# Row maxima off the diagonal by products of 64 rows in the two halves of the array, with the decay added on VectorE

## The chip, the cores and the metric

One core of one Trainium2 chip runs the whole program. The metric is the device time of one execution in microseconds; lower is better. Before the change it is 3023.38 us, the median of 3 runs (3023.07 to 3027.45).

## The reference, cut to what matters

Two decoder layers on a sequence of 2048 tokens, model width 1024: first a gated linear attention (GLA), then a forgetting attention (FoX) with 16 heads of width 64. The change lies in the second. For each head it computes, over all earlier keys,

```python
c = jnp.cumsum(log_f, axis=-1)
logits = (jnp.einsum('bhqd,bhkd->bhqk', qb, k).astype(jnp.float32) * scale
          + cb[..., :, None] - c[..., None, :])
mask = key_pos[None, :] <= q_pos[:, None]
probs = jax.nn.softmax(jnp.where(mask, logits, -jnp.inf), axis=-1)
return jnp.einsum('bhqk,bhkd->bhqd', probs.astype(v.dtype), v)
```

`log_f` is the logarithm of a forget gate, so `c` falls along the sequence. The softmax needs a number per query that is near the largest logit, to be subtracted ahead of the exponential. `c[t]` is the same for all keys of a query and drops out; what is left is the maximum over the keys of q.k - c[s].

## The kernel before, in words

**Tiling.** The sequence is cut into 4 blocks of 512 tokens (`T`, `NCH`). fp32 numbers are carried as two parts in a reduced fp32 format, high and low, and a dense product takes three matrix products (high x high, high x low, low x high). The second layer (from about 1100 us) runs block by block: projections, then for each of the 16 heads the maxima and the attention, then the output projection and a gated per-layer embedding.

**The maxima** (`maxima`, L1302). For block `c` and head `h` it goes over the key blocks `gk` = 0 to `c`, and in each over four query tiles `t` of 128. One product gives 128 queries x 512 keys: `E_` (128 x 512) is the stationary operand and `dk` the moving one. `E_` holds the high part of the queries in rows 0 to 63, ones in rows 64 and 65, and row 66 is filled later with the negative maximum; the rest is zero. `dk` holds the high part of the keys in rows 0 to 63 and the two parts of -c[s] in rows 64 and 65. So the product is q.k - c[s] at once. Off the diagonal (`gk < c`) VectorE reduces it with `tensor_reduce`; on the diagonal (`gk == c`) a fused add and maximum (`tensor_tensor_reduce`, in the profile CUSTOM_DVE_ANT_0 and a read of its accumulator) adds the mask `lim`. The four maxima per query are reduced, transposed on TensorE (`m4c` or `mx` with `ident`), negated and written by a DMA into row 66 of `E_`.

**The attention** (`attention`, L1364) uses the same `E_` again: for each tile of 128 keys one product of `B` (low and high part of the keys) with `A_` (high and low part of the queries) and one of `Dc` (rows as in `dk`, and a row of ones at 66) with `E_`. So the maximum comes off in the product. The exponentials follow on ScalarE, differences and sums on VectorE and GpSimd, and two products with `V`.

**Loads.** `load_d` (L1296) brings rows 64 to 129 of the scratch tensor `KS[gk][h]` (low part of the keys, high part, the two parts of the decay) into the 66 upper rows of one of two `Dm` (maxima) or two `Dc` (attention) tiles; `load_kv` (L1356) adds `B` and `V`. `forget` (L1220) computes the decay and stores its parts into `KS`. All DMAs are issued by SyncE (SP) in one queue.

**Order of the work.** Instructions are not emitted where they stand. A planner (`Streams`, L76) runs generators as streams with priorities: maxima 0.5, attention 2.5, dense work 3 (`P_M`, `P_A`, `P_D`, L60; the lower goes first). It keeps a clock of its own with a cost for each operation (`mm`, L397; `Engine`, L288), and a stream yields until operands, banks or marks are there by that clock. Each engine then executes in the planned order. The eight PSUM banks are handed out by `take` and `give`; `bank(keep)` (L252) waits until more than `keep` banks are free, and the maxima ask with `K_M` = 1. No product of the maxima is planned while the one before the last (`M_LIVE` = 2) is not yet reduced. `level(Q_M)` with 1 puts the reductions behind other work that VectorE could do.

**Weights** in the second layer come as already split halves of a matrix (`half`, L589: 12 products each) through `WB` + `WX` = 4 + 1 pairs of buffers (`wload`, L417); a load is issued when a pair falls free.

Every operation is recorded by one helper, so all rows of the trace have the line L180.

Of the kernel before, what the change touches and what calls it, by code (L numbers as in the profile page):

```python
# [20 lines left out]
P = 128  # L21
# [3 lines left out]
T = 512  # L25
# [8 lines left out]
PARTS = ("xnh", "xnl", "ogh", "ogl", "hr")  # L34


BANKS, K_D, K_V, K_M, M_LIVE = 8, 0, 0, 1, 2

PB, PF, PL, LAG = 3, 2, 3, 2

WR, WB, WX = 2, 4, 1

AB, A_STEP = 2, 8.0

# [9 lines left out]

G_OF = 2

Q_W, Q_C, Q_M = -1, 1, 1

Q_N = -1
P_A, P_M, P_D = 2.5, 0.5, 3  # L60
# [15 lines left out]
class Streams:  # L76
# [107 lines left out]
    @staticmethod  # L184
    def parts(ap):

        n = ap.tensor.name
        base = n.rsplit("_", 1)[0]
        if base in PARTS:
            first = ap.offset % (KT * T)  # L190
            last = first + sum((k - 1) * q for q, k in ap.ap[1:])
            return [(n, k) for k in range(first // T, last // T + 1)]
        if base[:2] == "KS":
            last = ap.offset + sum((k - 1) * q for q, k in ap.ap)
            return [(n, k) for k in range(ap.offset // (130 * T), last // (130 * T) + 1)]
        return [n]

    def over(self, ops):
# [117 lines left out]
def trunk_kernel(ctx: ExitStack, tc: tile.TileContext, a: dict, out: bass.AP, layers: int = 2):  # L316
# [77 lines left out]
    def t2(name, tag, bufs):  # L394
        return tmp.tile([P, T], F32, tag=tag, name=name, bufs=bufs)

    def mm(dst, w, x, start=True, stop=True):  # L397
        n = dst.free_size()
        sq_.op("P", [dst], [w, x], max(n, 64) * (4 if x.dtype == F32 or n < 256 else 1) / 2400.0 + 0.0134, partial(nc0.tensor.matmul, dst, w, x, start=start, stop=stop))

    def transpose(dst, src):
        sq_.op("P", [dst], [src], 0.107, partial(nc0.tensor.transpose, dst, src, ident))
# [1 line left out]
    def rdma(dst, src):  # L404
        nc.sync.dma_start(dst.bitcast(F32), src.bitcast(F32))
# [758 lines left out]
    def setup1():  # L1164
        sq_.flush()
        gx.close()
        f, fc = sbuf("f", 2), sbuf("fc", 1)
        L["f"] = f
        free.extend([fc.tile([P, 4, P], F32R, name=f"wx{x}{i}") for x in "hl"] for i in range(WX))

        L["onesb"] = fc.tile([P, P], F32R, name="onesb")
        onesb = L["onesb"].bitcast(F32)
        nc.vector.memset(onesb, 0.0)
        nc.vector.memset(onesb[0:64, 0:64], 1.0)
        nc.vector.memset(onesb[64:128, 64:128], 1.0)
        L["onesh"] = onesh = fc.tile([P, 2, P], F32, name="onesh")
        nc.vector.memset(onesh, 0.0)
        nc.vector.memset(onesh[:, 0, 0:64], 1.0)
        nc.vector.memset(onesh[:, 1, 64:128], 1.0)

        L["lim"] = lim = fc.tile([P, T + P], BF16, name="lim")
        nc.vector.memset(lim, 0.0)
        nc.vector.memset(lim[:, T:], -BIG)
        nc.gpsimd.affine_select(lim[:, T - P : T], lim[:, T - P : T], pattern=[[-1, P]], compare_op=ALU.is_ge, fill=-BIG, base=0, channel_multiplier=1)
        L["limT"] = limT = fc.tile([P, 2 * P], BF16, name="limT")
        nc.vector.memset(limT, 0.0)
        nc.gpsimd.affine_select(limT, limT, pattern=[[1, 2 * P]], compare_op=ALU.is_ge, fill=-BIG, base=-P, channel_multiplier=-1)
        L["qkg"] = qkg = fc.tile([P, 2], F32, name="qkg")
        nc.sync.dma_start(qkg, a["qkgain"])
        nc.vector.tensor_scalar(qkg[:, 0:1], qkg[:, 0:1], -(HD ** -0.5), None, ALU.mult)  # L1190
        nc.vector.tensor_scalar(qkg[:, 1:2], qkg[:, 1:2], -1.0, None, ALU.mult)
        L["bf"] = bf = fc.tile([FH, 1], F32, name="bf")
        nc.sync.dma_start(bf, a["fox_bf"])
        wfr = t2("wfr", "sq", 2)[:, 0 : KT * FH].rearrange("p (k n) -> p k n", n=FH)
        nc.sync.dma_start(wfr, a["fox_wf"])
        L["wf"] = wf = fc.tile([P, KT, 48], F32R, name="wf")
        nc.vector.memset(wf.bitcast(F32), 0.0)
        split(wf[:, :, 0:16], wf[:, :, 32:48], wfr, nc.vector)

        L["As"] = [fc.tile([P, T], F32R, name=f"As{i}") for i in range(NQ)]
        L["Es"] = [fc.tile([P, T], F32R, name=f"Es{i}") for i in range(NQ)]
        L["Dm"] = [fc.tile([P, T], F32R, name=f"Dm{i}") for i in range(2)]
        L["Dc"] = [fc.tile([P, T], F32R, name=f"Dc{i}") for i in range(2)]
        for t in (*L["Es"], *L["Dm"], *L["Dc"]):
            nc.vector.memset(t[64:128].bitcast(F32), 0.0)
        for t in L["Dc"]:
            rdma(t[66:67].rearrange("o (t n) -> o t n", n=P), ones[0:4])
        for t in L["Es"]:  # L1210
            nc.vector.memset(t[64:66].bitcast(F32), 1.0)
        L["carry"] = fc.tile([FH, 1], F32, name="carry")
        nc.vector.memset(L["carry"], 0.0)

        L["KS"] = [dram.tile([FH, 130, T], F32R, name=f"KS{c}") for c in range(NCH)]

        L["QS"] = [[dram.tile([P, T], F32R, name=f"QS{h}_{c}") for c in range(NCH)] for h in range(FH)]
        L["VS"] = [[dram.tile([8, P, 4, P], F32R, name=f"VS{i}_{c}") for c in range(NCH)] for i in range(2)]

    def forget(c):  # L1220
# [19 lines left out]
        nc.vector.scalar_tensor_tensor(cl, e, -1.0, ch.bitcast(F32), ALU.mult, ALU.subtract)  # L1240
        rdma(L["KS"][c][:, 128], ch)
        rdma(L["KS"][c][:, 129], cl)

    def qk_unit(c, u, col):

# [50 lines left out]
    def load_d(h, gk, kind):  # L1296
        d = L[kind][nd[kind] % len(L[kind])]
        nd[kind] += 1
        rdma(d[0:66], L["KS"][gk][h, 64:130])
        return d  # L1300

    def maxima():  # L1302

        done = []
        for i in range(NCH * FH):
# [3 lines left out]
            if i >= NQ:  # L1309
                yield ("S", i - NQ)  # L1310
            A_, E_ = L["As"][i % NQ], L["Es"][i % NQ]
            rdma(E_[0:64], L["QS"][h][c][0:64])
            rdma(A_, L["QS"][h][c])
            dk = load_d(h, 0, "Dm")
            mx = L["f"].tile([P, 4, NCH], F32, tag="mx", name="mx")
            for gk in range(c + 1):
                nxt = load_d(h, gk + 1, "Dm") if gk < c else None
                for t in range(4):
                    yield both(at(E_, dk), done[-M_LIVE] if len(done) >= M_LIVE else lambda: 0.0)
                    yield bank(K_M)  # L1320
                    n = T if gk < c else max(256, (t + 1) * P)
                    pm = psa("pm")
                    mm(pm[:, :n], E_[:, t * P : (t + 1) * P], dk[:, :n])
                    m1 = mx[:, t, gk : gk + 1]
                    with level(Q_M):
                        if gk < c:
                            nc.vector.tensor_reduce(m1, pm, AX.X, ALU.max)
                        else:
                            l0 = T - (t + 1) * P
                            nc.vector.tensor_tensor_reduce(pm[:, :n], pm[:, :n], L["lim"][:, l0 : l0 + n], 1.0, -BIG, ALU.add, ALU.max, accum_out=m1)  # L1330
                    give(pm)
                    done.append(at(mx))
                    yield
                dk = nxt
            if c:
                m4 = L["f"].tile([P, 4], F32, tag="m4c", name="m4c")
                nc.vector.tensor_reduce(m4, mx[:, :, : c + 1], AX.X, ALU.max)
# [6 lines left out]
            mr = L["f"].tile([4, P], F32R, tag="mr", name="mr")  # L1344
            nc.scalar.mul(mr, pt[0:4, 0:P], -1.0)
            give(pt)
            rdma(E_[66:67].rearrange("o (t n) -> o t n", n=P), mr)
            mark(("C", i))

    pend = []  # L1350
# [2 lines left out]
    def both(f, g):  # L1353
        return lambda: max(f(), g())
# [289 lines left out]
```

## Time and profile before

| what | value |
|---|---|
| median of 3 runs | 3023.38 us |
| the profiled execution, its time | 3025.52 us |
| its span, first to last instruction | 3023.8 us |
| granted TensorE clock, mean | 0.994 of full speed |
| TensorE busy | 2970.6 us (98%) |
| VectorE / ScalarE / GpSimd busy | 2134.2 / 1905.4 / 1330.8 us |
| moved by DMA | 648.15 MB, 66.5% of 16 engines |

Rows name an engine (PE is TensorE, PEld its loads of weights, DVE VectorE, ACT ScalarE, POOL GpSimd, SP the DMA queue), then what is written and read by the program's names without buffer numbers; every PSUM tile is called `bank`. Products are given as rows*columns of the weights and the shape of the moving operand.

### The profile page before, as it was taken

The numbers are of one execution on the slowest core, as the hardware profiler recorded it, in microseconds if no ns is written. First come the engines' busy times: TensorE is split into PE (matmuls) and PEld (weight loads), VectorE is DVE, ScalarE is ACT, GpSimd is POOL, SyncE is SP. The second block draws the span as 40 slices with busy tenths as digits, with TensorE's granted clock in tenths as the row PEclk, the third lists the DMA queues.
The fourth block names the chain that finished last, engine by engine and source line by source line (L and its number), as shares of the span: only waits on it lengthen the run. The fifth ranks groups of instructions, "written<-read, shape, count | busy, mean of one in ns | idle before, by whom it ended". The sixth has DMA issues, their size and how long they took to land.

```text
span 3023.8 us, 43646 instructions
## 1 busy us (share of the span) xinstructions
PE 2970.6 (98%) x13568; PEld 2406.8 (80%) x13568; DVE 2134.2 (71%) x3824; ACT 1905.4 (63%) x3651; POOL 1330.8 (44%) x1097
## 2 busy tenths in 40 slices
PE   8999999999999999999899999999999999999998
PEld 6887887888788888887788777778777788777876
DVE  7687668668765765675764877774787768798845
ACT  6666666657565465664555756565776657667745
POOL 1232222213222234453543645553776647677741
PEclk9999999999999999999999999999999999999999
DMA  5565657556642568887668777667776777766665
GB/s 193 180 212 192 203 195 244 196 186 228 209 143 81 179 196 250 276 268 248 218 220 270 236 247 246 213 211 257 226 219 224 230 238 233 227 190 210 196 228 159
DMA packets 379738, 648.15 MB, mean 214 GB/s; under 512 B 43097, under 2 KB 78433, under 8 KB 379506
## 3 DMA queue, kind: packets, MB, share of 16 engines
q1 hardware_dynamic: 379506, 645.37, 66.5%
q8 instruction: 108, 1.77, 0.2%
q14 instruction: 124, 1.02, 0.1%
HBM read 521.86 MB, written 123.21 MB: 213 GB/s over the span
## 4 chain that ended last, share of the span: by engine, by line
PE 90%; DVE 3%; ACT 3%; DMA 2%; issue 1%; POOL 0%; SPq 0%; DVEq 0%; ACTq 0%; POOLq 0%
PE bank L180 90%; ACT rs L180 1%; DMA B<-KS 1%; DVE wl L180 0%; DVE hr L180 0%; DMA Dm<-KS 0%; DMA wr<-gla_wv 0%; DVE ny L180 0%; ACT Ph L180 0%; DVE bank L180 0%; SPq L180 0%; DVE rs L180 0%; POOL Pl L180 0%; DMA ar<-fox_wg 0%; DMA hr<-hs 0%
## 5 line engine op out<-in xcount | busy, mean ns | idle before, releaser
L180 ACT ACTIVATE Ph<-bank 128x512 fp32r<-128x512 f32 (+2 forms) x640 | 339.0, 545 | 131.1 <-PE bank L180 64.2
L180 DVE TENSOR_TENSOR wl<-wr,wh 128x512 fp32r<-128x512 f32 x332 | 253.4, 770 | 149.8 <-ACT wh L180 120.7
L180 PE MATMUL bank<-xnh,wh 128*128 128x512 f32 (+1 forms) x1184 | 338.7, 393 | 0.3 <-DVE ny L180 0.2
L180 PE MATMUL bank<-xnh,wl 128*128 128x512 f32 (+1 forms) x1184 | 337.7, 392 | 0.0
L180 PE MATMUL bank<-xnl,wh 128*128 128x512 f32 (+1 forms) x1184 | 333.0, 391 | 0.0
L180 DVE TENSOR_REDUCE mx<-bank 128x1 f32<-128x512 f32 x384 | 253.2, 684 | 79.4 <-PE bank L180 76.7
L180 ACT CAST wh<-wr 128x512 fp32r<-128x512 f32 x332 | 202.6, 615 | 106.4 <-PE bank L180 63.1
L180 DVE TENSOR_TENSOR Pl<-bank,Ph 128x512 fp32r<-128x512 f32 (+1 forms) x320 | 194.2, 607 | 106.4 <-ACT bank L180 95.4
L180 POOL TENSOR_TENSOR ag<-ag,Pf 128x512 f32<-128x512 f32 x192 | 226.4, 1179 | 79.2 <-ACT Pf L180 57.1
L180 PEld LDWEIGHTS bank<-xnh,wh 128*128 128x128 f32 x1184 | 220.3, 188 | 47.3 <-issue 1.1
L180 PEld LDWEIGHTS bank<-xnh,wl 128*128 128x128 f32 x1184 | 220.6, 188 | 45.7 <-issue 0.6
L180 PEld LDWEIGHTS bank<-xnl,wh 128*128 128x128 f32 x1184 | 219.9, 188 | 45.0 <-issue 0.9
L180 PE MATMUL bank<-ogh,wh 128*128 128x512 f32 x856 | 242.3, 393 | 5.2 <-ACT ogh L180 2.6
L180 PE MATMUL bank<-As,B 128*128 128x512 f32 (+2 forms) x640 | 241.1, 377 | 3.2 <-DMA B<-KS 1.0
L180 PE MATMUL bank<-ogl,wh 128*128 128x512 f32 x856 | 241.3, 393 | 0.3
L180 PE MATMUL bank<-ogh,wl 128*128 128x512 f32 x856 | 240.6, 392 | 0.0
L180 PE MATMUL bank<-Pl,V 128*128 128x512 f32 (+2 forms) x640 | 235.9, 369 | 2.8 <-POOL Pl L180 2.0
L180 PE MATMUL bank<-Ph,V 128*128 128x512 f32 (+2 forms) x640 | 235.0, 367 | 0.0
L180 PE MATMUL bank<-Es,Dc 128*128 128x512 f32 (+2 forms) x640 | 234.7, 367 | 0.0
L180 PE MATMUL bank<-Dm,Es 128*128 128x512 f32 (+2 forms) x640 | 231.1, 378 | 3.0 <-DMA Dm<-KS 2.4
L180 POOL TENSOR_TENSOR Pl<-Pf,Ph 128x512 fp32r<-128x512 f32 x192 | 228.8, 1197 | 2.7 <-ACT Ph L180 2.1
L180 PEld LDWEIGHTS bank<-ogh,wh 128*128 128x128 f32 x856 | 160.2, 189 | 40.3 <-ACT ogh L180 3.6
(271 smaller groups left out, 7072.8 us busy)
## 6 DMA issues: line engine op xcount, KB each, us to landing
B<-KS SPq DMA_DIRECT2D x160, 256.0 KB
V<-VS SPq DMA_DIRECT2D x160, 256.0 KB
Dm<-KS SPq DMA_DIRECT2D x160, 132.0 KB
Dc<-KS SPq DMA_DIRECT2D x160, 132.0 KB
wr<-gla_wv SPq DMA_DIRECT2D x64, 256.0 KB
wr<-gla_wqk SPq DMA_DIRECT2D x64, 256.0 KB
wr<-gla_wg SPq DMA_DIRECT2D x64, 256.0 KB
wr<-gla_wo SPq DMA_DIRECT2D x64, 256.0 KB
```

The costliest lines, as they stand in the source:

```text
L180: q.emit()
```

## The change

Off the diagonal two query tiles are taken together. The queries of one lie in rows 0 to 63 of `A_` (the high part, loaded there for the attention anyway), those of the other in rows 64 to 127 of `E_`; so `E_` and `dk` are turned over: high parts in rows 64 to 127, ones, decay and maximum in rows 0 to 2. `dk` gets the high part of the keys in both halves. Each product then has 64 rows, and the two use different halves of the array and different banks. They hold q.k alone; -c[s] is stored once per block in fp32 (`CS`), loaded as a tile broadcast to 128 partitions (`cb`, two buffers), and added by the fused add and maximum. Diagonal tiles stay as they are, but their loads, and those of the attention, take two DMAs in place of one. `KS` has a 131st row of zeros. To make room for `cb` the fifth pair of weight buffers goes (`WX` = 0). `M_LIVE`, `K_M` and `Q_M` change, and the planner counts the second product of a pair as 0.01 us.

```diff
-BANKS, K_D, K_V, K_M, M_LIVE = 8, 0, 0, 1, 2
+BANKS, K_D, K_V, K_M, M_LIVE = 8, 0, 0, 0, 3
...
-WR, WB, WX = 2, 4, 1
+WR, WB, WX = 2, 4, 0
...
-Q_W, Q_C, Q_M = -1, 1, 1
+Q_W, Q_C, Q_M = -1, 1, 0
...
-    def mm(dst, w, x, start=True, stop=True):
+    def mm(dst, w, x, start=True, stop=True, beside=0):
         n = dst.free_size()
-        sq_.op("P", [dst], [w, x], max(n, 64) * (4 if x.dtype == F32 or n < 256 else 1) / 2400.0 + 0.0134, partial(nc0.tensor.matmul, dst, w, x, start=start, stop=stop))
+        sq_.op("P", [dst], [w, x], 0.01 if beside else max(n, 64) * (4 if x.dtype == F32 or n < 256 else 1) / 2400.0 + 0.0134, partial(nc0.tensor.matmul, dst, w, x, start=start, stop=stop))
...
-            nc.vector.memset(t[64:128].bitcast(F32), 0.0)
+            nc.vector.memset(t[0:64].bitcast(F32), 0.0)
         for t in L["Dc"]:
-            rdma(t[66:67].rearrange("o (t n) -> o t n", n=P), ones[0:4])
+            rdma(t[2:3].rearrange("o (t n) -> o t n", n=P), ones[0:4])
...
-        L["KS"] = [dram.tile([FH, 130, T], F32R, name=f"KS{c}") for c in range(NCH)]
+        L["KS"] = [dram.tile([FH, 131, T], F32R, name=f"KS{c}") for c in range(NCH)]
+        for c in range(NCH):
+            rdma(L["KS"][c][:, 130], L["Dm"][0][0:FH])
+
+        L["CS"] = [dram.tile([FH, T], F32, name=f"CS{c}") for c in range(NCH)]
...
+        nc.vector.tensor_scalar(lf, e, -1.0, None, ALU.mult)
+        nc.sync.dma_start(L["CS"][c], lf)
...
     def load_d(h, gk, kind):
         d = L[kind][nd[kind] % len(L[kind])]
         nd[kind] += 1
-        rdma(d[0:66], L["KS"][gk][h, 64:130])
+        rdma(d[64:128], L["KS"][gk][h, 64:128])
+        n = 3 if kind == "Dm" else 2
+        rdma(d[0:n], L["KS"][gk][h, 128 : 128 + n])
         return d
+
+    def load_m(c, h, gk):
+
+        if gk == c:
+            return load_d(h, gk, "Dm"), None
+        d = L["Dm"][nd["Dm"] % len(L["Dm"])]
+        nd["Dm"] += 1
+        for i in range(2):
+            rdma(d[64 * i : 64 * i + 64], L["KS"][gk][h, 64:128])
+        cb = L["f"].tile([P, T], F32, tag="cb", name="cb", bufs=2)
+        nc.sync.dma_start(cb, L["CS"][gk][h : h + 1].to_broadcast([P, T]))
+        return d, cb
...
-            rdma(E_[0:64], L["QS"][h][c][0:64])
+            rdma(E_[64:128], L["QS"][h][c][0:64])
             rdma(A_, L["QS"][h][c])
-            dk = load_d(h, 0, "Dm")
+            nxt = load_m(c, h, 0)
...
             for gk in range(c + 1):
-                nxt = load_d(h, gk + 1, "Dm") if gk < c else None
+                dk, cb = nxt
+                nxt = load_m(c, h, gk + 1) if gk < c else None
+                if gk < c:
+
+                    for t in (0, 2):
+                        yield both(both(at(E_, dk), at(A_, cb)), done[-M_LIVE] if len(done) >= M_LIVE else lambda: 0.0)
+                        pms = []
+                        for j in range(2):
+                            yield bank(K_M * (1 - j))
+                            pms.append(psa("pm"))
+                        for j, q in enumerate((A_, E_)):
+                            js = slice(64 * j, 64 * j + 64)
+                            mm(pms[j], q[js, (t + j) * P : (t + j + 1) * P], dk[js], beside=j)
+                        for j, pm in enumerate(pms):
+                            with level(Q_M):
+                                nc.vector.tensor_tensor_reduce(pm, pm, cb, 1.0, -BIG, ALU.add, ALU.max, accum_out=mx[:, t + j, gk : gk + 1])
+                            give(pm)
+                            done.append(at(mx))
+                        yield
+                    continue
...
-            rdma(E_[66:67].rearrange("o (t n) -> o t n", n=P), mr)
+            rdma(E_[2:3].rearrange("o (t n) -> o t n", n=P), mr)
```

## Rows read from the trace of the kernel before

**Rows 1.** The page, part 1: busy time, share of span, instructions.

```profile
PE 2970.6 (98%) x13568; PEld 2406.8 (80%) x13568; DVE 2134.2 (71%) x3824; ACT 1905.4 (63%) x3651; POOL 1330.8 (44%) x1097
```

**Rows 2.** The page, part 4: the chain that ended last, by engine.

```profile
PE 90%; DVE 3%; ACT 3%; DMA 2%; issue 1%; POOL 0%; SPq 0%; DVEq 0%; ACTq 0%; POOLq 0%
```

**Rows 3.** Stretches: length, busy time of each engine, TensorE clock, DMA share, GB/s.

```profile
1180.00:2900.00 1720.00, 1700.66 (x7599) 1362.44 (x7597) 1246.73 (x2490) 1116.15 (x2236) 993.81 (x823) 1.00 0.74 232
2500.00:2800.00 300.00, 296.57 (x1321) 237.42 (x1320) 258.77 (x486) 214.60 (x431) 216.66 (x176) 1.00 0.69 214
```

**Rows 4.** Timeline of TensorE from 2003.96 us: start, time, engine, operation, count.

```profile
2003.96 0.39 PE L180 MATMUL bank<-Pl,V 128*128 128x512 f32 x1
2003.96 0.42 PEld L180 LDWEIGHTS bank<-Dm,Es 128*128 128x128 f32 x2
2004.19 0.62 PE L180 MATMUL bank<-Dm,Es 128*128 128x512 f32 x2
...
2004.65 0.40 PE L180 MATMUL bank<-As,B 128*128 128x512 f32 x1
```

**Rows 5.** VectorE's groups by form: count, busy us, mean ns, idle before.

```profile
L180 DVE TENSOR_REDUCE mx<-bank 128x1 f32<-128x512 f32 x384 | 253.2, 684 | 79.4 <-PE bank L180 76.7
...
L180 DVE SCALAR_TENSOR_TENSOR rs<-bank,rs 128x512 f32<-128x512 f32 x127 | 87.1, 686 | 1.6
...
L180 DVE CUSTOM_DVE_ANT_0 bank<-bank,lim 128x512 f32<-128x512 f32 x64 | 44.6, 697 | 5.3 <-PE bank L180 5.0
...
L180 DVE DVE_READ_ACCUMULATOR2_ANT mx<- 128x1 f32 x256 | 35.7, 139 | 0.2
```

**Rows 6.** TensorE's groups by form: products of the maxima with 512 columns.

```profile
L180 PE MATMUL bank<-Dm,Es 128*128 128x512 f32 x448 | 173.4, 407 | 2.9 <-DMA Dm<-KS 2.4 <-ACT rs L180 0.4
```

**Rows 7.** Timeline of the weight loads from 1808.43 us, beside products of 256 columns.

```profile
1808.43 0.19 PEld L180 LDWEIGHTS bank<-Es,Dc 128*128 128x128 f32 x1
1808.55 0.19 PEld L180 LDWEIGHTS bank<-Ph,V 128*128 128x128 f32 x1
1808.67 0.19 PEld L180 LDWEIGHTS bank<-Pl,V 128*128 128x128 f32 x1
```

**Rows 8.** Timeline of TensorE around weights of 48 and of 4 columns.

```profile
1806.11 1.79 PE L180 MATMUL bank<-xnh,wf 128*48 128x512 f32 x7
1807.74 0.40 PE L180 MATMUL bank<-Ph,V 128*128 128x512 f32 x1
...
1920.66 0.39 PE L180 MATMUL bank<-Pl,V 128*128 128x512 f32 x1
...
1920.89 0.27 PE L180 MATMUL bank<-ident,m4c 128*4 128x128 f32 x1
...
1920.92 0.36 PE L180 MATMUL bank<-As,B 128*128 128x256 f32 x1
```

**Rows 9.** Instructions on tile mx: the plain reductions, ns, first and last start.

```profile
L180 DVE TENSOR_REDUCE mx<-bank x384: 672/681/693, 1422.8 to 2854.7; 128x1 f32<-128x512 f32 x192
```

**Rows 10.** DMA queue (packets, MB, share), issues with KB, and issue times (ns).

```profile
q1 hardware_dynamic: 379506, 645.37, 66.5%
...
Dm<-KS SPq DMA_DIRECT2D x160, 132.0 KB
Dc<-KS SPq DMA_DIRECT2D x160, 132.0 KB
...
L180 SPq DMA_DIRECT2D Dm<-KS x160: 288/350/1011, 1097.7 to 2845.3; - x160
```

**Rows 11.** TensorE's waits for the maxima's keys; DMA pieces of the chain (start, us).

```profile
  DMA Dm<-KS: 4.8, 4
...
1922.74 7.08 DMA Dm<-KS
2391.22 5.24 DMA wl<-fox_wv_0l
2396.48 6.95 DMA B<-KS
```

More of the change, by code (lines that the diff above doesn't have):

```diff
@@ L194, in parts @@
             last = ap.offset + sum((k - 1) * q for q, k in ap.ap)
-            return [(n, k) for k in range(ap.offset // (130 * T), last // (130 * T) + 1)]
+            return [(n, k) for k in range(ap.offset // (131 * T), last // (131 * T) + 1)]
         return [n]
@@ L1206, in setup1 @@
         for t in (*L["Es"], *L["Dm"], *L["Dc"]):
-            nc.vector.memset(t[64:128].bitcast(F32), 0.0)
+            nc.vector.memset(t[0:64].bitcast(F32), 0.0)
         for t in L["Dc"]:
-            rdma(t[66:67].rearrange("o (t n) -> o t n", n=P), ones[0:4])
+            rdma(t[2:3].rearrange("o (t n) -> o t n", n=P), ones[0:4])
         for t in L["Es"]:
-            nc.vector.memset(t[64:66].bitcast(F32), 1.0)
+            nc.vector.memset(t[0:2].bitcast(F32), 1.0)
         L["carry"] = fc.tile([FH, 1], F32, name="carry")
         nc.vector.memset(L["carry"], 0.0)
-        L["KS"] = [dram.tile([FH, 130, T], F32R, name=f"KS{c}") for c in range(NCH)]
+        L["KS"] = [dram.tile([FH, 131, T], F32R, name=f"KS{c}") for c in range(NCH)]
+        for c in range(NCH):
+            rdma(L["KS"][c][:, 130], L["Dm"][0][0:FH])
+        L["CS"] = [dram.tile([FH, T], F32, name=f"CS{c}") for c in range(NCH)]
         L["QS"] = [[dram.tile([P, T], F32R, name=f"QS{h}_{c}") for c in range(NCH)] for h in range(FH)]
@@ L1320, in maxima @@
                     yield bank(K_M)
-                    n = T if gk < c else max(256, (t + 1) * P)
+                    n = max(256, (t + 1) * P)
                     pm = psa("pm")
                     mm(pm[:, :n], E_[:, t * P : (t + 1) * P], dk[:, :n])
-                    m1 = mx[:, t, gk : gk + 1]
                     with level(Q_M):
[L1326 to L1330, printed above, removed]
+                        l0 = T - (t + 1) * P
+                        nc.vector.tensor_tensor_reduce(pm[:, :n], pm[:, :n], L["lim"][:, l0 : l0 + n], 1.0, -BIG, ALU.add, ALU.max, accum_out=mx[:, t, gk : gk + 1])
                     give(pm)
@@ L1333, in maxima @@
                     yield
-                dk = nxt
             if c:
```

## The prediction

> **What bounds the kernel now.** I read the shares of the engines first, then the chain of work that ended last, then the stretches. TensorE is busy 98% of the span with 13,568 products and every other engine is well below it [rows 1]; the chain is 90% TensorE, and VectorE, ScalarE, the DMAs and plain issue hold about a tenth of it between them [rows 2]. The stretch from 1180 to 2900 us, where the changed work lies, shows the same: TensorE 1700.7 of 1720 us, VectorE 1246.7, the DMA engines 74% [rows 3]. The one place where a second engine comes near is 2500 to 2800 us: VectorE 258.8 of 300 us [rows 3]. A busy TensorE need not be a full one, so I looked at the distance between starts: a 512-column product occupies its slot for 0.23 us, although its own record is 0.39 us long [rows 4]; the rest of the record runs beside the next product. 13,568 products in 2970.6 us are 0.219 us each, so the engine is close to its own rate and fewer slots should mean less time. The clock is at its upper level in all of it (1.00 in both stretches of [rows 3]).
>
> All durations below are of the profiled execution: its time is 3025.52 us, 2.1 us above the median of 3023.38. What a run of this kernel can tell from no change is about 0.2%, 6 us.
>
> **1. The products.** Off the diagonal there are 384 of them: that is the count of plain reductions [rows 5], and the 448 products of 512 columns are these and the 64 last tiles of diagonals [rows 6]. 384 x 0.23 = 88 us of TensorE. They become 192 pairs of products with 64 rows, one in the upper and one in the lower half of the array. No product of the trace has fewer than 128 rows, so a pair has to be bounded.
> - *Best:* both run side by side and a pair takes one slot: 192 x 0.23 = 44 us less.
> - *Weights decide:* each half still loads its own 128 columns of weights. Where products are short (256 columns), products with a load each follow each other every 0.12 us [rows 7], so a load needs no more than that. If the second half's load starts only when the first product has started, the pair takes 0.12 + 0.23 = 0.35 us instead of 0.46: 0.11 x 192 = 21 us less.
> - *Nothing overlaps:* 0.
> - *Worse:* on each change between whole and half array the running product must end first, which is its record less its slot, 0.39 - 0.23 = 0.16 us, twice per pair: 0.23 + 0.32 = 0.55 us against 0.46, 17 us more; without any overlap on top of it 61 us more.
>
> I take 0.27 us per pair, 0.04 above one slot. Two loads at 0.12 us fit into the slot of the product ahead, which starts a load at its own start [rows 4], so the value lies nearer the best end. Saved: (0.46 - 0.27) x 192 = 36.5 us, all on the path.
>
> Does a change of the array's shape cost? The trace has a relative of it in the other direction, columns: seven products with 48 columns of weights start at 1806.11, and the next with 128 at 1807.74, 0.233 us each with both changes in it; the transposition with 4 columns starts 0.23 us after its forerunner and the next product 0.03 us after it [rows 8]. No change shows 0.16 us. The Trainium skill says otherwise: "TensorEngine Tiling (Array Packing)", section "Tiling Modes" (Key Properties), states that changing the tiling mode drains TensorE, and by it the sum would be the worse end above. The trace does not agree for columns; for rows no run here shows it. The other page, "TensorE: Matmul & The Clock Gate" (Part 3), starts packed products about 4 ns apart; by that a pair would cost almost exactly one slot and the sum would come out some 7 us lower.
>
> **2. VectorE.** A plain reduction is 684 ns. The diagonal already does the new form, add and maximum in one pass: 697 ns for 128x512, and 139 ns to read the accumulator [rows 5]. So 836 - 684 = 152 ns more, x384 = 58 us. The second operand is now fp32 and not bf16; a pass over 512 fp32 elements of a bank with an fp32 tile from SBUF is 686 ns [rows 5], so that costs nothing. The cover is TensorE's chain: VectorE goes from 1247 to about 1305 of 1720 us. VectorE holds 3% of the chain with 71% busy, 91 of 2134 us or 4%: 58 x 0.04 = 2.5 us. In 2500 to 2800 us the cover is thin: 86% busy already, and the new work (its share by time is 12 us, 300/1432 of 58, from 1423 to 2855 us [rows 9]) brings it to 90%. Half of those 12 us on the path would be 6. I take 4 us, between 0 and 10. The price falls on those queued behind a longer pass, chiefly ScalarE's exponentials, which wait for VectorE's mask on the diagonal.
>
> **3. DMAs and SP's queue.** 96 key blocks lie off the diagonal. Each now loads 2 x 128 KB of keys instead of 132 KB, and 256 KB for the broadcast decay: 380 KB x 96 = 37 MB on 645 MB [rows 10], all inside 1720 us at 74%; that takes the DMA engines to about 81%. The queue gains 96 second halves, 96 broadcasts, a second short load for each of 160 attention blocks and 64 diagonal blocks, and 8 stores: 424 issues of about 0.35 us [rows 10], 148 us in a queue whose issues are in order; weights and value tiles queue behind them. A key load takes some 7 us when the queue is full, and TensorE waited 4 times, 4.8 us in all, for one [rows 11]. With a tenth more traffic and each head's first key block some 0.7 us later in the queue (two more issues), I take 4 us; bounds 0, where the loads stay ahead as now, and 12, where the 48 heads with blocks off the diagonal each wait 0.25 us more.
>
> **4. One weight buffer less.** Five pairs of buffers become four in the second layer. Each serves 12 products, 12 x 0.23 = 2.8 us of unbroken dense work, so a load that starts when a buffer falls free has 3 x 2.8 = 8.3 us instead of 11 before its first use. Loads that are waited for took 5.2 to 7.1 us [rows 11]; 8.3 still covers that, barely, and attention lies between the dense products. I take 3 us; 0 where the cover holds, 10 where one in ten of the layer's 400 halves of a weight matrix (100 for each of four blocks, by the code) comes 0.25 us late.
>
> **5. The bookkeeping.** Looser limits on banks (a third reduction may be pending, no bank is kept back) and a planner that counts the second half of a pair as 0.01 us reorder the whole second layer. I put this at 0, within 5 either way. Setup (fills, four 32 KB zero rows) lies ahead of the layer once: under 1 us.
>
> **Sum.** -36.5 + 4 + 4 + 3 = -25.5 us: 3000 for the profiled execution, 2998 against the median.
>
> **Rivals.**
> - *The array empties at each change* (slower). The place is the first product of each pair and the first after it; it decides from 0.115 us per change on, where 0.23 + 2 x 0.115 = 0.46 eats the whole gain. At 0.16 us: 17 + 11 (points 2 to 4) = 28 us more, 3051. For it: no 64-row product was ever timed here. Against it: the narrow products [rows 8]. Chance 0.11. The skill's page on tiling, named above, is on this side.
> - *The halves do not run side by side*, so the change does not do what it says: 0 + 11, 3034. For it: the products stay two instructions in one stream. Chance 0.11.
> - *Weights decide*: -21 + 11, 3013. For it: loads are single file in the trace. Chance 0.13.
> - *The gain turns into waits*: TensorE is relieved, and VectorE's 2500 to 2800 us, the weights and the key loads pay their upper bounds, 10 + 12 + 10 = 32 us, which leaves 3019 at 36.5 saved. Chance 0.10.
> - The forecast: 0.55, 2978 to 3010.
>
> **How the numbers follow.** The low end is the best pair with the side costs at nothing, 3023.4 - 44 = 2979, and a little for the order, 2977; the high end takes in the halves that do not overlap, 3034, and leaves out the emptying array. Faster by over 0.2%: forecast and weights, less a little, 0.66. Slower: the first two rivals, 0.22. Within: the fourth and what the others leave, 0.12.
>
> **What would show it.** Right: products with 64 rows that start in twos a few hundredths of a us apart, the next whole product some 0.27 us after the first; VectorE about 58 us busier; TensorE's busy time in 1423 to 2855 us down by 30 to 40 us; TensorE's waits for DMA no more than a few us longer. Wrong: a gap of 0.1 us or more at the edges of each pair (emptying); second halves 0.12 us (weights) or 0.23 us (no overlap) behind the first; TensorE idle behind weights or maxima.

## The result and the profile after

The changed kernel takes 3215.61 us (median of 4 runs, 3209.07 to 3221.69) against 3025.20 for the kernel before on the same chip: 1.063 times as long, 95% interval 1.0618 to 1.0642. That is 190 us slower, on the other side of the forecast and far above its range. The profiled execution took 3218.49 us.

First the page of the changed kernel: busy time of each engine, the DMA queue, the chain by engine, and three groups of DMA issues.

```profile
PE 3066.8 (95%) x13568; PEld 2391.1 (74%) x13568; DVE 2140.5 (67%) x4212; ACT 1907.6 (59%) x3651; POOL 1322.3 (41%) x1097
...
q1 hardware_dynamic: 402962, 682.61, 68.0%
...
PE 79%; DMA 6%; DVE 5%; ACT 4%; issue 3%; POOL 3%; SPq 1%; DVEq 0%; POOLq 0%; ACTq 0%
...
Dm<-KS SPq DMA_DIRECT2D x256, 128.0 KB
cb<-CS SPq DMA_DIRECT2D x96, 256.0 KB
Dc<-KS SPq DMA_DIRECT2D x160, 128.0 KB
```

Against [rows 1]: the span grew by 193 us, from 3023.8 to 3216.8. TensorE's busy time grew by 96 us, and the time in which it does nothing from 53 to 150 us, another 97. No other engine works noticeably longer: VectorE has 2140.5 us against 2134.2. Against [rows 2] the chain lost 11 points of TensorE, and they went to everything at once: DMA (2 to 6%), POOL (0 to 3%), DVE (3 to 5%) and plain issue (1 to 3%). So the answer is not one engine that became too busy. The DMA engines carry the predicted 37 MB more (682.6 against 645.4 in [rows 10]) in a longer span.

The same stretches as in [rows 3] (length, busy time of each engine, TensorE's clock, DMA share, GB/s), then the mean clock of the whole span:

```profile
1180.00:2900.00 1720.00, 1624.97 (x6890) 1222.75 (x6889) 1130.89 (x2577) 997.60 (x1998) 866.99 (x725) 0.97 0.77 233
2500.00:2800.00 300.00, 283.77 (x1187) 207.67 (x1184) 215.00 (x486) 181.14 (x360) 172.70 (x140) 0.98 0.79 237
```

```profile
core 0: 3216.8 us, clock 0.977
```

In the same 1720 us TensorE does 6890 products where it did 7599. The clock was 0.994 of full speed over the span before and is 0.977 now. Of 3216.8 us that is (1 - 0.977) x 3216.8 = 74 us lost to the lower of the two levels (1.2 GHz in place of 2.4), against (1 - 0.994) x 3023.8 = 18 us before: up to 56 of TensorE's 96 us of additional busy time can be products that ran at the lower level.

**Who is waited for.** The two largest sums of TensorE's waits ahead of products on tile Dm, by what ended them (us, times):

```profile
  DMA Dm<-KS: 21.1, 16
  DVE mx L180: 13.7, 14
```

Before, TensorE's products waited 2.4 us for these loads, in 2 waits ([rows 6]; the 4.8 us in 4 waits of [rows 11] count the idle time ahead of the loads of weights too). DMAs of all kinds now end 42 us of TensorE's waits, 3 us before; most of the rest of the 97 us is ended by other engines, VectorE (39 against 17) and GpSimd (23 against 2) first. In the chain of waits 15 pieces of over 4 us are now loads of keys (the list of before names two of them, one in [rows 11]), 87 us in all against 12.5. One of the 15 (start, us, what), and TensorE at its end (in brackets idle time and what ended it):

```profile
2026.27 7.56 DMA Dm<-KS
```

```profile
2030.94 0.50 PE L180 MATMUL bank<-Dm,As 64*128 64x512 f32 x1
2033.87 0.49 PE L180 MATMUL bank<-Dm,Es 64*128 64x512 f32 x1 [2.43 <-DMA Dm<-KS]
```

The first product of the pair needs the half of the key tile that is loaded first, the second product the other half. Of TensorE's 16 waits for keys 14 stand, like this one, ahead of the second product of a head's first pair, and none ahead of the first.

**The place.** These loads sit where one head's maxima end and the next head's begin. SP's queue at such a place (start, us):

```profile
2082.70 0.45 SPq L180 DMA_DIRECT2D Dm<-KS  x1
2083.25 0.53 SPq L180 DMA_DIRECT2D cb<-CS  x1
2083.88 0.66 SPq L180 DMA_DIRECT2D Es<-mr  x1
...
2086.69 1.03 SPq L180 DMA_DIRECT2D Dm<-KS  x1
```

TensorE there, the last 512-column maxima product of the old head and the first of the new one:

```profile
2077.62 0.39 PE L180 MATMUL bank<-Dm,Es 128*128 128x512 f32 x1
...
2091.51 0.50 PE L180 MATMUL bank<-Dm,As 64*128 64x512 f32 x1
```

The first half of the key tile is issued at 2082.70, the second 4.0 us later at 2086.69, and the head's first product follows 13.9 us after the last one of the head before. The queue issued six other DMAs between the two. The reason stands in the planner's `Streams.op`: `Dm` is one operand for it, and a DMA ("H") that writes an operand is planned behind the landing of an earlier DMA that writes it,

```python
deps[o] = self.AFTER[o.e] if o.e != e or e == "H" else 0.0
```

What used to be one load of 66 rows is now two loads in series. I measured this gap, from the start of the last maxima product of a head to the first of the next, at all 45 such boundaries of blocks 1 to 3 (a head of block c has 4(c+1) of these products in a row): the median went from 9.3 to 15.0 us and the sum from 616 to 828 us.

**The pairs.** TensorE around one pair, products and loads of weights (start, us):

```profile
1995.55 0.84 PE L180 MATMUL bank<-xnl,wh 128*128 128x512 f32 x3
1996.32 0.50 PE L180 MATMUL bank<-Dm,As 64*128 64x512 f32 x1
1996.32 0.50 PE L180 MATMUL bank<-Dm,Es 64*128 64x512 f32 x1
1996.75 0.50 PE L180 MATMUL bank<-xnl,wh 128*128 128x512 f32 x1
1997.09 1.09 PE L180 MATMUL bank<-xnh,wl 128*128 128x512 f32 x4
```

```profile
1996.32 0.18 PEld L180 LDWEIGHTS bank<-Dm,As 64*128 64x128 f32 x1 [0.35 <-DVE ny L180]
1996.32 0.18 PEld L180 LDWEIGHTS bank<-Dm,Es 64*128 64x128 f32 x1
1996.75 0.19 PEld L180 LDWEIGHTS bank<-xnl,wh 128*128 128x128 f32 x1 [0.25 <-issue]
1996.86 0.89 PEld L180 LDWEIGHTS bank<-xnh,wl 128*128 128x128 f32 x4
```

The halves do run side by side: both start at 1996.32. But their weights are loaded at 1996.32 too, and those of the next whole product at 1996.75, with their own products; before, a load began one slot early [rows 4]. Both are the rule: in the median a load starts 2 ns ahead of its product for a pair behind whole products and for a whole product behind a pair, and 224 ns ahead for a whole product behind another. Over all 192 pairs the medians are: product ahead to pair 0.319 us, half to half 0.004, pair to the next product 0.422, and from that to the one after it 0.338. From the product ahead of the pair to the second behind it that is 1.089 us. Four whole products in a row take 4 x 0.23 = 0.92. A pair costs about 0.16 us more than the two products that it replaces, not 0.19 less.

### The profile page after: what moved, and what is told of

It is laid out like the page before. It is cut to its first block, busy times and chain, and to the rows that moved or that the text cites. A ratio compares the mean times of both kernels' runs of the same rounds, so it can differ in the third digit from the quotient of the medians.

```text
span 3216.8 us, 44816 instructions
## 1 busy us (share of the span) xinstructions
PE 3066.8 (95%) x13568; PEld 2391.1 (74%) x13568; DVE 2140.5 (67%) x4212; ACT 1907.6 (59%) x3651; POOL 1322.3 (41%) x1097
## 4 chain that ended last, share of the span: by engine, by line
PE 79%; DMA 6%; DVE 5%; ACT 4%; issue 3%; POOL 3%; SPq 1%; DVEq 0%; POOLq 0%; ACTq 0%
PE bank L180 79%; DMA Dm<-KS 3%; POOL Pl L180 1%; DVE bank L180 1%; ACT Ph L180 1%; SPq L180 1%; DVE ny L180 1%; POOL ag L180 1%; ACT rs L180 1%; DMA wh<-ple_gate_1h 0%; ACT bank L180 0%; DVE hr L180 0%; DVE wl L180 0%; POOL ogl L180 0%; ACT sq L180 0%
## 5 line engine op out<-in xcount | busy, mean ns | idle before, releaser
L180 PE MATMUL bank<-xnh,wh 128*128 128x512 f32 (+1 forms) x1352 | 387.7, 395 | 2.8 <-DVE ny L180 2.0
L180 PE MATMUL bank<-xnl,wh 128*128 128x512 f32 (+1 forms) x1352 | 384.8, 394 | 0.0
L180 PE MATMUL bank<-xnh,wl 128*128 128x512 f32 (+1 forms) x1352 | 384.0, 394 | 0.0
L180 DVE CUSTOM_DVE_ANT_0 bank<-bank,cb 128x512 f32<-128x512 f32 x384 | 260.3, 703 | 92.5 <-PE bank L180 90.0
L180 PEld LDWEIGHTS bank<-xnh,wh 128*128 128x128 f32 x1352 | 252.4, 189 | 60.4 <-issue 4.7
L180 PEld LDWEIGHTS bank<-xnl,wh 128*128 128x128 f32 x1352 | 251.8, 189 | 56.2 <-issue 6.0
L180 PEld LDWEIGHTS bank<-xnh,wl 128*128 128x128 f32 x1352 | 251.6, 189 | 54.8 <-issue 4.2
L180 PE MATMUL bank<-ogh,wh 128*128 128x512 f32 x960 | 272.2, 397 | 6.4 <-ACT wh L180 2.6
L180 PE MATMUL bank<-ogl,wh 128*128 128x512 f32 x960 | 269.7, 394 | 0.3
L180 PE MATMUL bank<-Es,Dc 128*128 128x512 f32 (+2 forms) x640 | 243.5, 381 | 15.6 <-DMA Es<-mr 11.7
L180 PEld LDWEIGHTS bank<-ogl,wh 128*128 128x128 f32 x960 | 180.1, 189 | 41.0 <-issue 2.2
```

Source lines behind the costliest of these rows:

```text
L180: q.emit()
```

## The experiments

The runs began with four theories: the planner's new rules, the pairs, the traffic, or the missing weight buffer makes it slow. VectorE's pass joined them at run 4 and the late keys at run 8. All ratios are to the kernel before on the same chip.

**1. Rules of before in the changed kernel.**

```diff
-K_M, M_LIVE = 0, 3      Q_M = 0
+K_M, M_LIVE = 1, 2      Q_M = 1
```

> The changed kernel with the old rules of the planner (K_M 1, M_LIVE 2, Q_M 1), all else as changed. Theory rules (TensorE stalls because the planner hands out the last bank and VectorE is late with it): at least half of the 190 us comes back, 3120 us or less. Theories pair, traffic and weight buffer: within 30 us of the changed kernel's 3216.

3312.78 us, 1.0956 (1.0922 to 1.0989): 97 us worse than the change, outside both expectations. With the rest of the change in place, the new rules are the better ones.

**2. The kernel before without the fifth pair of weight buffers.**

```diff
-WR, WB, WX = 2, 4, 1
+WR, WB, WX = 2, 4, 0
```

> The kernel before with four pairs of weight buffers in place of five, nothing else. Theory weight buffer: it takes a large part of the 190 us, 3080 us or more. The other theories: at most 20 us more than before, 3045 or less.

3018.40 us (8 runs), 0.9976 (0.9964 to 0.9987): 7 us faster. The buffer was worth nothing.

**3. Whole products in the changed kernel.** Loads, broadcast and fused pass stay; the products have 128 rows again, over a key tile whose lower half is zeros.

```diff
-rdma(d[64 * i : 64 * i + 64], L["KS"][gk][h, 64:128])
+rdma(d[64 * i : 64 * i + 64], L["KS"][gk][h, 64:128] if i else L["ZS"])
...
-mm(pms[j], q[js, (t + j) * P : (t + j + 1) * P], dk[js], beside=j)
+mm(pms[j], E_[:, (t + j) * P : (t + j + 1) * P], dk)
```

> The changed kernel with the pair undone: each off-diagonal tile is one product of 128 rows again (the lower half of the keys' tile is loaded from zeros, so loads, the added decay, buffers and rules stay as changed), and the planner counts both products in full. Theory pair (emptying the array, and a planner that reckons with 0.01 us for the second half): 3100 us or less, below the changed kernel although 44 us of slots come back. Theories rules, traffic, weight buffer: 3216 + up to 44 us, 3210 to 3260.

3242.38 us, 1.0723 (1.0671 to 1.0774): 27 us slower still. So the pairs are not what costs 190 us. In this trace the four slots around two products measure 0.928 us in the median, as they should, but 1.47 us in the mean with their waits (1.42 with the pairs): at these places waits outweigh slots.

**4 to 7. The parts one by one.** Run 4 is the kernel before with `WX` = 0 and the new rules alone. Run 5 adds the turned layout and its split loads (64 rows and 2 or 3 rows by two DMAs), with whole products and the plain reduction. Runs 6 and 7 each add one thing to run 5: the fused pass with a tile of zeros, or the traffic (an unread broadcast of 256 KB and 128 KB of keys per block off the diagonal).

```diff
-nc.vector.tensor_reduce(m1, pm, AX.X, ALU.max)
+nc.vector.tensor_tensor_reduce(pm, pm, L["zf"], 1.0, -BIG, ALU.add, ALU.max, accum_out=m1)
...
+rdma(L["du"][0:64], L["KS"][gk][h, 64:128])
+cb = L["f"].tile([P, T], F32, tag="cb", name="cb", bufs=2)
+nc.sync.dma_start(cb, L["CS"][gk][h : h + 1].to_broadcast([P, T]))
```

> The kernel before with four pairs of weight buffers and the new rules (K_M 0, M_LIVE 3, Q_M 0), nothing else. Theory rules (they are a cost by themselves, which the rest of the change needs): 3040 us or more, against 3018 with the old rules. Theories pass and traffic: 3010 to 3030.

> As the run with the new rules alone, and the turned-over layout with each load of Dm and Dc in two DMAs (128 KB and 2 or 3 rows of 2 KB) as in the changed kernel; products of 128 rows with the decay in them, plain reductions, no broadcast tile. Theory traffic, in its part queue (more issues in SP's queue): 30 us or more above the run with the rules alone. Theory pass: within 10 us of it.

> As the run with split loads, but off the diagonal the add and maximum in one pass (with a constant tile of zeros) in place of the plain reduction: 58 us more for VectorE, no more traffic. Theory pass: at least half of the 224 us between 3018 and 3242 (whole products) comes here, 3130 us or more. Theory traffic: 3080 or less.

> As the run with split loads, plain reductions, but for each of the 96 key blocks off the diagonal also the broadcast load of 256 KB and a second load of 128 KB, which nothing reads. Theory traffic: at least half of the 224 us comes here, 3130 us or more. Theory pass: 3080 or less.

| run | us | ratio (95%) | against |
|---|---|---|---|
| 4, rules | 3059.53 | 1.0105 (1.0076 to 1.0134) | +41 on run 2 |
| 5, split loads | 3069.46 | 1.0138 (1.0108 to 1.0167) | +10 on run 4 |
| 6, fused pass | 3126.20 | 1.0325 (1.0295 to 1.0355) | +57 on run 5 |
| 7, traffic | 3137.90 | 1.0364 (1.0334 to 1.0394) | +68 on run 5 |

Run 6 missed the 3130 us of its theory by 4 us and run 7 reached it, where one of the two was expected at 3080 or less: neither theory rules the other out. One by one: -7 + 41 + 10 + 57 + 68 = 169; the pair in place of whole products gives 27 back (run 3), 142, and 48 more come from the parts being there together. No part explains it alone, and the parts are not independent of the order: the gap between heads is 11.7 us in run 4 and 14.6 to 14.9 in runs 5 to 7, from 9.4 in run 2. In run 5 it is as long as in the change, and costs 10 us over run 4.

**8 and 9. Keys earlier.** Run 8 only makes the planner stricter (`K_M` = 1, the second product of a pair counted as 0.28 us). Run 9 adds that the next head's first keys and broadcast are asked for while the present head is on its diagonal block.

```diff
-            nxt = load_m(c, h, 0)
+            nxt = nxt or load_m(c, h, 0)
...
-                nxt = load_m(c, h, gk + 1) if gk < c else None
+                nxt = load_m(c, h, gk + 1) if gk < c else load_m(c, h + 1, 0) if c and h + 1 < FH else None
```

> The changed kernel with K_M 1, M_LIVE 3, Q_M 0, and the planner told 0.28 us for the second half of a pair. It is the reference of the next run. Theory false price (the plan went wrong because it reckoned with 0.01 us): 3185 or less, against 3216. Theory late keys: 3200 or more, since the loads stay where they are.

> As the run before it, and the keys (and the broadcast decay) of the next head's first key block are loaded already while the diagonal block of the present head is at work. Theory late keys (the maxima of a head wait for loads that got slower and more, and everything behind them in the fixed order waits too): 60 us or more below the run before it. Theories pass and bytes (VectorE's work and the moved bytes are what costs): within 25 us of it, since both stay the same.

Run 8: 3237.47 us, 1.0703 (1.0656 to 1.0750), 22 us slower than the change: the truer price in the plan and the stricter `K_M` together bring nothing back (they were not tried apart). Run 9: 3102.61 us, 1.0257 (1.0223 to 1.0292). Asking for the keys and the broadcast earlier, nothing else, takes 135 us off run 8, with the same bytes (683 MB in the queue) and the same pairs. The gap between heads falls from 15.6 to 9.7 us, and TensorE's waits ahead of products on Dm become (us, times):

```profile
  DMA Dm<-KS: 14.1, 11
  DMA As<-QS: 4.3, 5
...
  DVE mx L180: 0.3, 1
```

TensorE's idle time falls from 168.3 us in run 8 to 92.5, and the clock, 0.972 there, returns with it:

```profile
core 0: 3097.5 us, clock 0.992
```

**10. The split with the old rules**, run 5 with `K_M`, `M_LIVE`, `Q_M` = 1, 2, 1.

> The run with split loads alone (3069), but with the old rules (K_M 1, M_LIVE 2, Q_M 1). Theory late keys: the split costs far more under the rules that hold less in flight, 3100 or more. Theory that rules and split add up: 3018 + 10 = 3028, within 10.

3142.69 us, 1.0390 (1.0360 to 1.0420): two DMAs in place of one, with no other part of the change but the layout, `WX` and the small stores of `CS`, cost 3142.7 - 3018.4 = 124 us. Under the new rules (run 5 against run 4) the same split cost 10.

**11. Two pairs in a row** (one profile, no rounds): four query tiles of a key block together, so that the second pair follows the first without a change of shape.

```diff
-for t in (0, 2):
+for t in (0,):
...
+yield bank(3)
-for j, q in enumerate((A_, E_)):
+for j, q in enumerate((A_, E_, A_, E_)):
```

> The changed kernel with all four tiles of a key block in two pairs one right behind the other (four banks at once). For the spacing of the products alone, not for the total. If the array empties only where its shape changes: the second pair starts some 0.23 us behind the first, and the 0.32 and 0.42 us stand only ahead of the first pair and behind the second. If every pair costs: 0.3 us or more between the pairs.

3337.25 us in its one run. An undisturbed place of it:

```profile
2008.49 0.39 PE L180 MATMUL bank<-Pl,V 128*128 128x512 f32 x1
2008.81 0.50 PE L180 MATMUL bank<-Dm,As 64*128 64x512 f32 x1
2008.81 0.50 PE L180 MATMUL bank<-Dm,Es 64*128 64x512 f32 x1
2009.14 0.39 PE L180 MATMUL bank<-Dm,As 64*128 64x512 f32 x1
2009.15 0.39 PE L180 MATMUL bank<-Dm,Es 64*128 64x512 f32 x1
2009.47 0.50 PE L180 MATMUL bank<-As,B 128*128 128x512 f32 x1
```

It is 0.32 us ahead of the first pair, 0.33 between the pairs and 0.32 behind. The 0.33 is what was expected if every pair costs: a pair's step is not one slot of 0.23, also behind another pair. Yet the loads of the second pair do start ahead, with the pair in front of it:

```profile
2008.91 0.19 PEld L180 LDWEIGHTS bank<-Dm,As 64*128 64x128 f32 x1
2008.91 0.19 PEld L180 LDWEIGHTS bank<-Dm,Es 64*128 64x128 f32 x1
```

So a load comes late where the number of rows changes, and the 0.33 us between pairs has another reason, which no run shows. From the product ahead of the two pairs to the second behind them it is 1.335 us in the median of 90 such places, against 6 x 0.23 = 1.38 for whole products: two pairs in a row about break even, where a single one loses 0.16.

**12. Run 9 with whole products** (edit of run 3).

> The run with the next head's keys loaded ahead (3103), but with whole products of 128 rows in place of the pairs; loads, pass and rules the same. Theory that a pair takes about the slots of two whole products: within 15 us of 3103. Theory that a pair saves 0.19 us each, as forecast: 3140 or so.

3114.87 us, 1.0291 (1.0270 to 1.0311). The pairs are worth 12 us here, 27 in run 3, while their undisturbed slots are 192 x 0.16 = 31 us longer; the intervals of runs 9 and 12 overlap. The two kernels have different plans and waits (TensorE idles 92.5 us in run 9, 115.0 in run 12), so neither number is a price of the pair itself.

**13 and 14. Early keys without the pairs:** runs 5 and 6 with the edit of run 9.

> The run with split loads alone (3069), with the next head's first keys loaded ahead. Theory late keys: below 3069, at 3050 or less. Rival: no change, since with few bytes the loads are in time.

> The run with the longer pass on VectorE (3126), with the next head's first keys loaded ahead. If the pass cost so much only because the keys were late as well: at most 25 us above the run with split loads and keys ahead. If VectorE's work counts in full by itself: 45 to 65 us above it.

Run 13: 3086.25 us, 1.0196 (1.0176 to 1.0216), which missed: 17 us slower than run 5 although its gap falls from 14.9 to 10.8 us. Run 14: 3087.63 us, 1.0201 (1.0180 to 1.0221). The fused pass costs 1.4 us on top of run 13, where it cost 57 on top of run 5. The same instructions, then, cost nothing in one order and 57 us in another; the cost is not VectorE's work.

**15. Early keys in the kernel before** (with `WX` = 0).

> The kernel before with four pairs of weight buffers (3018) and the next head's first keys loaded ahead. Theory late keys holds for the kernel before too: 3010 or less. Rival: within 6 us of 3018, since with one short load per key block the keys come in time.

3014.45 us (5 runs), 0.9961 (0.9947 to 0.9976). This is the fastest of all, ahead of both kernels, but not the 3010 that late keys would have given; the rival, within 6 us of 3018, came true: in run 2 TensorE waits only 3.3 us for keys. Against run 2 it gains 4 us, and the two intervals overlap, so of the two edits only the buffer is shown.

**16 to 18. The two loads not in series.** The planner gets the two 64-row halves of `Dm` and `Dc` as operands of their own (`parts`), so that the second half needn't wait for the first: in the change itself (16), in run 10 (17), in run 9 (18).

```diff
+        if base[:2] in ("Dm", "Dc"):
+            last = ap.offset + sum((k - 1) * q for q, k in ap.ap)
+            return [(n, k) for k in range(ap.offset // (64 * T), last // (64 * T) + 1)]
```

> The changed kernel, with only the planner's bookkeeping altered: the upper and lower 64 rows of Dm and Dc count as separate operands, so that the second load of a tile need not be planned behind the landing of the first. Theory serial halves: 3170 or less, against 3216. Theory bytes and pass (the time is lost to traffic and VectorE's work): within 20 us of 3216.

> The run with split loads under the old rules (3143), with the halves counted as separate. Theory serial halves: 3060 or less. Theory queue (each extra issue in SP's queue costs by itself): within 25 us of 3143.

> The pair with the keys loaded ahead under K_M 1, M_LIVE 3, Q_M 0 (3103), with the halves counted as separate. Theory serial halves: 20 us or more below 3103. Theory that loading ahead has already hidden them: within 15 us of 3103.

| run | us | ratio (95%) | against |
|---|---|---|---|
| 16 | 3161.26 | 1.0448 (1.0417 to 1.0478) | -54 on the change |
| 17 | 3054.04 | 1.0093 (1.0064 to 1.0123) | -89 on run 10 |
| 18 | 3070.24 | 1.0147 (1.0117 to 1.0176) | -32 on run 9 |

SP's queue at a boundary of run 16, between the last 512-column product of a head at 2049.19 and the next head's first at 2058.86:

```profile
2054.30 1.12 SPq L180 DMA_DIRECT2D Dm<-KS  x2
2055.52 0.53 SPq L180 DMA_DIRECT2D cb<-CS  x1
2056.09 1.08 SPq L180 DMA_DIRECT2D Dm<-KS  x2
```

The halves are issued side by side. In the chain of run 16 no piece is a load of `Dm`, where the change has 87 us of them. The gap between heads falls from 15.0 to 12.2 us (16), from 13.6 to 9.1 (17) and from 9.7 to 9.9, that is not at all, in 18. Two limits of these runs: the edit frees the halves of `Dc` too (TensorE's waits for its loads are 1.0 us in the change), and every such edit reorders the whole layer. In run 10 TensorE's own waits for `Dm` are only 7.5 us and in run 17 still 7.0, so the 89 us that run 17 takes back come from the other order; which part of it is not shown. Run 18 is the best with pairs, and still 45 us slower than the kernel before:

```profile
PE 2999.3 (98%) x13568; PEld 2358.0 (77%) x13568; DVE 2147.5 (70%) x4212; ACT 1904.6 (62%) x3651; POOL 1326.2 (43%) x1097
```

```profile
core 0: 3067.9 us, clock 0.994
```

At the clock of the kernel before, TensorE is busy 28.7 us longer than in [rows 1] and idle 68.6 us against 53.2. The 31 us of longer slots at the pairs would account for the first; that is arithmetic, not a run that takes them away.

## Why the prediction was wrong

**Point 3, the DMAs, is the step that failed.** "I take 4 us; bounds 0, where the loads stay ahead as now, and 12, where the 48 heads ... each wait 0.25 us more." I counted bytes and issues and asked if the queue had room; it did (68.0% of the DMA engines). I didn't follow the one path that has no room: last maximum of a head, load, first maximum of the next. The planner puts a second DMA into a tile behind the landing of the first, and I took both halves as issued together ("some 0.7 us later in the queue (two more issues)"; it is 4.0 us at the place above). Of the 45 measured boundaries 40 became longer; the median rose by 5.7 us and the sum by 212, where I had allowed 0.25 per head. Runs 9 and 16 show that this is a cost: keys asked for earlier (-135) and halves not in series (-54); run 17 does the second where no pair is present (-89). The gap alone does not set the time: in run 5 its sum is that of the change, 828 us, and the run is 146 us faster; there loads of `Dm` are 0.6% of the chain, in the change 2.7%. So the 54 us of run 16 are the part of the 190 that is shown for the halves in series, with `Dc`'s among them; how the rest divides among rules, pass, traffic and their common order stays open.

What is lost there doesn't stay there: every engine runs in an order fixed ahead of time, so TensorE stands while work that could be done is queued behind the waiting product. Here is such a follow-on wait, TensorE and then VectorE of the changed kernel:

```profile
2002.41 0.50 PE L180 MATMUL bank<-Dm,As 64*128 64x512 f32 x1 [0.68 <-ACT Ph L180]
2007.03 0.79 PE L180 MATMUL bank<-Dm,Es 64*128 64x512 f32 x1 [4.12 <-DVE mx L180]
```

```profile
2002.89 3.42 DVE L180 SCALAR_TENSOR_TENSOR ny<-hr,gcol,rs 128x512 f32<-128x512 f32 x2
2006.23 0.68 DVE L180 CUSTOM_DVE_ANT_0 bank<-bank,cb 128x512 f32<-128x512 f32 x1
```

The second half of a pair waits 4.1 us for its bank, because the pass that frees it is ordered behind two others that take 3.42 us in all. In this wait the clock falls; the 10.2 us from 2005.30 (columns as in [rows 3]) are at its lower level, 0.50:

```profile
2005.30:2015.50 10.20, 6.13 (x15) 4.60 (x16) 10.20 (x22) 5.10 (x9) 4.69 (x4) 0.50 0.25 75
```

Of TensorE's 96 us of additional busy time up to 56 are the clock and 31 the slots of the pairs; 9 are left.

**Point 1, the products.** "I take 0.27 us per pair." The halves start 3 to 4 ns apart, so the two run side by side. The Trainium skill, "TensorE: Matmul & The Clock Gate" (Part 3), starts packed products about 4 ns apart; the trace agrees. The failed part is "two loads at 0.12 us fit into the slot of the product ahead": they don't start there. The loads for the pair and the load behind it begin with their own products, and the three starts around a pair come 0.09, 0.19 and 0.11 us later than a slot of 0.23 would have it; that the late loads are the whole cause isn't shown, since the load for the third of these products does start ahead. A pair takes 0.62 us where I had 0.27, above even my worst value with the halves side by side (0.55). Undisturbed that is +31 us in place of -36.5. The rival of the emptying array named the right place and a price of 0.16 us twice, 0.32 per pair; measured are 0.39 over the three starts. The trace before showed no cost at changes of columns [rows 8], and I carried that to rows, where it doesn't hold. The page I weighed against it, "TensorEngine Tiling (Array Packing)", section "Tiling Modes" of the Trainium skill, states that a change of tiling mode drains TensorE; for rows the trace agrees with it in direction, with 0.39 us over the three starts. By that rule alone a step between two pairs, where no mode changes, would be one slot; run 11 has 0.33 us there, with the loads ahead of it.

**Point 2, VectorE.** The 58 us of work were never there. I added the record of the pass and the record of the accumulator's read, 697 + 139 ns. The changed kernel's groups have about those values (count, busy us, mean ns, idle before):

```profile
L180 DVE CUSTOM_DVE_ANT_0 bank<-bank,cb 128x512 f32<-128x512 f32 x384 | 260.3, 703 | 92.5 <-PE bank L180 90.0 <-DMA wh<-ple_gate_0h 2.1
...
L180 DVE DVE_READ_ACCUMULATOR2_ANT mx<- 128x1 f32 x640 | 88.9, 139 | 0.2
```

But the timeline of VectorE shows the read beside the next pass. First the changed kernel, then a plain reduction of the kernel before:

```profile
2009.37 0.68 DVE L180 CUSTOM_DVE_ANT_0 bank<-bank,cb 128x512 f32<-128x512 f32 x1
2009.98 0.13 DVE L180 DVE_READ_ACCUMULATOR2_ANT mx<- 128x1 f32 x1
2009.98 0.68 DVE L180 TENSOR_TENSOR acc<-bank,acc 128x512 f32<-128x512 f32 x1
```

```profile
2007.46 0.68 DVE L180 TENSOR_REDUCE mx<-bank 128x1 f32<-128x512 f32 x1
2008.06 0.68 DVE L180 TENSOR_TENSOR Pl<-bank,Ph 128x512 fp32r<-128x512 f32 x1
```

From start to start it is 0.61 us against 0.60, and busy VectorE rose by 6 us in all. I had read slots from starts on TensorE and not on VectorE. The 4 us I took (0 to 10) hold where keys are early (1.4, run 14); the 57 of run 6 come with another plan of the same instructions. The planner books the fused pass 0.17 us dearer than a reduction (L307), which moves everything behind it; whether that price alone makes the 57 I did not try.

**Point 4, the weight buffer:** +3 forecast, -7 measured (run 2). Loads have cover enough with four.

**Point 5, bookkeeping:** "0, within 5 either way" failed as well. The rules alone cost 41 us (run 4), and in the changed kernel the old rules cost 97 us more (run 1). A reordering of a whole layer can't be bounded by its own small size.

**The rivals.** "The gain turns into waits" was right in kind and put the waits where they are, at key loads among others, but priced them at 32 us in all. All of them lay between 3013 and 3051 us; none was built from how long a head takes to hand over to the next.

**Open:** what the rest of run 18 is (45 us over the kernel before, of which the slots of the pairs would be 31); why early keys made run 13 slower by 17 us; why the split costs 124 us under the old rules and 10 under the new ones.

## What to carry to other kernels

Where every engine runs in an order fixed ahead of time, a step that is cheap in work can be dear in latency: follow each moved or split load from what allows it to who waits for it, and look for the one hand-over with no slack, before adding up bytes and busy shares. Read slots from start to start on every engine; records that overlap can't be added. Two half-array products cost more than two whole ones where they stood alone among whole products, and about broke even two pairs in a row, so time a pair among the products that will surround it before rearranging data for it.

## What the runs showed of the hardware

- Two 64-row products in the two halves of the array start 3 to 4 ns apart, and the next pair 0.33 us later. Where products change between 128 and 64 rows, weights are loaded with their own product; between whole products (224 ns ahead in the median) and between pairs (228 ns ahead, run 11) they are loaded under the product ahead.
- The cost of a single pair reaches two products further: the first whole product behind it comes 0.42 us later, and the one after that another 0.34.
- The read of VectorE's accumulator (0.13 us) lies wholly beside the next instruction: 0.61 us from start to start with it, 0.60 without it for a reduction (medians 0.616 and 0.601).
- The kernels in which TensorE waited longer also ran longer at the lower level of its clock: up to 74 us lost to it with 150 us idle (the change), 18 us with 53 and 69 us idle (before, and run 18: (1 - 0.994) x 3067.9).
